# Seven weight splits moved from VectorE to accumulating DMAs, and the last heads of yB0 in another order

## The chip, the core and the metric

The kernel runs on one core of one Trainium2 chip. The core has five engines with queues of their own: TensorE (PE, matrix products; its weight loads are listed as PEld), VectorE (DVE), ScalarE (ACT), GpSimd (POOL) and SyncE (SP). Each engine works through its queue in order and waits where a semaphore tells it to. Transfers are started from a queue (here SP's, POOL's and at the very start ACT's) and then run on the core's 16 DMA engines. The metric is the time of one execution on the device in microseconds (us).

## What is computed

One layer of a block with two attention branches and a convolutional feed-forward part, on 512 tokens of width 1024, all in float32.

```python
hn = rms_norm(x, norm1_g)
proj = hn @ w_in                       # [512,1024] @ [1024,5120]
out_a = chunked_attention(qa, ka, va, q_norm_g, k_norm_g, rel_bias)   # 8 heads x 64
out_b = stick_breaking_attention(qb, kb, vb)                          # 8 heads x 64
mixed = sigmoid(gate_a) * (out_a @ w_branch_a) + sigmoid(gate_b) * (out_b @ w_branch_b)
x = x + mixed @ w_out
x = x + conv_glu(rms_norm(x, norm2_g), w_ffn_up, ffn_conv_w, ffn_conv_b, w_ffn_down)

def conv_glu(x, w_up, conv_w, conv_b, w_down):   # D_FF = 2816
    hid = causal_depthwise_conv_width_3(x @ w_up) + conv_b
    gate, up = hid[..., :D_FF], hid[..., D_FF:]
    return (silu(gate) * up) @ w_down
```

## The kernel before

**Products in three parts.** Every float32 product is built from float32r matmuls, a type with fewer bits. Each operand is split into a high half (the value cast to float32r) and a low half (the value minus its high half, cast again). `mm3` (L310) then adds three matmuls in one PSUM bank: high by high (L312), and the two mixed ones (L313, L314). So each weight has to be split on the core before TensorE can use it.

**Weights as chunks.** All weights go through one list of chunks (`CHUNKS`): the parts of `w_in`, then `yA` and `yB` (the two branch outputs, two chunks each), `wo0` to `wo3`, then `up0` to `up21` and the down projection `dn`. A chunk of up weights is a pair: 128 gate columns and the 128 up columns that belong to them, 1 MB. `load` (L124) fetches a chunk with a DMA on SP into a raw buffer [128 x 2048], of which there are two. `split_gen` (L257) splits it: ACT casts the raw weights into `whi` (L281), and DVE subtracts that from the raw weights into `wlo` (L286). In the up stage this is done in two pieces of 128 x 1024. There are two `whi` and two `wlo` buffers. When the split of chunk i is through, the load of chunk i+2 is started, into the raw buffer just read.

`run_chunk` (L301) interleaves a chunk's body with the split of the next chunk. The code order is not the order in which the engines get their instructions: a scheduler places each one by a model of how long things take, as early as its operands and buffers allow in that model, and by priority. `behind(a, b)` forbids that a is placed ahead of b on its engine; `high_priority` pulls instructions forward. So a change of engine or of modelled time for one step can reorder other engines, too.

**The second branch's last heads.** Stick-breaking attention (branch B) is done in pairs of heads. `pv` (L786) multiplies probabilities by values into a PSUM tile, then ACT copies half of it (L800), DVE adds the halves together (L801), ACT casts the result of a pair of heads into `oh_B` (L805), and DVE makes its low half `ol_B` (L806). Pairs are named by their second head: B1, B3, B5, B7. `yB_body` (L874) multiplies the four pairs by a chunk of `w_branch_b`: through `feat_groups` (L593), four groups (yB0_0 to yB0_3) of 128 features, each 4 x 3 matmuls of 512 columns in a bank of the kind MM, of which there are three. `evac` reads a finished group: DVE multiplies it by the gate `gb` (L882), adds the other branch, ACT and DVE split the sum.

**The up stage.** Three kinds of pairs. Pairs 0 and 1 run while their tokens still come in. Nine pairs (`SEVEN` = 6, 7, 9, 10, 11, 12, 13, 15, 17) run as `up_seven` (L1139): seven products of block sums in place of eight products of blocks, 84 matmuls of 256 columns (L1151), named p1 to p7. Their third to fifth weight sums were split ahead of time, parked in DRAM and are fetched by SP (`fetch_extra` L225) into `wxh` and `wxl`, or for some pairs into the buffers `w20` and `w21`. The other eleven are plain (`up_body` L1078): 48 matmuls of 512 columns through `up_mm` (L991), 24 into the bank `pg` (gate), 24 into `pu` (up); after each half ACT applies a tap of the convolution (L986) and DVE adds two more, then silu, product and, for every second pair, sums of the results for the down projection.

**POOL's queue.** In the up stage POOL does no arithmetic. It issues seven stores `ayd` of 768 KB (L1076, one after every second pair) and, from pair 18 on, the fetches `ay` of the same data (L1105).

Before the first real product, nine matmuls on a constant tile (L362, `warm`) run at the kernel's start.

Of the kernel before, what the change touches and what calls it, by code (L numbers as in the profile page):

```python
# [8 lines left out]
F32 = mybir.dt.float32  # L9
# [66 lines left out]
def block_kernel(ctx: ExitStack, tc: tile.TileContext, x, xt, params, g2, rbx, wts, wd0, wd1, out):  # L76
# [180 lines left out]
    def split_gen(i, pieces):  # L257

        if i >= len(order):
            return  # L260
        key = order[i]
        kn = CHUNKS[i][1]
        raw = raws.pop(i)
        if i - pos["up0"] in LATE and i - pos["up0"] not in LIVE:
            fetch_extra(i - pos["up0"])
        sh = 48 if key[:2] in ("qA", "kA", "vB") else 16 if key in ("up0", "up1") or is_seven(i) else 0
        n = 512 * kn if i >= FIRST_DN else 2048
        hi = wp.tile([P, 2112], F32R, tag="whi", name=f"whi_{key}")[:, sh:sh + n]
        lo = wp.tile([P, 2112], F32R, tag="wlo", name=f"wlo_{key}")[:, sh:sh + n]
        splits[key] = (hi.rearrange("p (k c) -> p k c", k=kn), lo.rearrange("p (k c) -> p k c", k=kn))  # L270
        if i >= FIRST_DN:
            yield from split_down(i - FIRST_DN, raw, hi, lo)
        elif is_seven(i):
            yield from split_seven(i, raw, hi, lo)
        n = 2048 // pieces
        cuts = CUTS[0] if i == 0 else [n * j for j in range(pieces + 1)] if i < FIRST_DN and not is_seven(i) else ()
        for j, sl in enumerate(map(slice, cuts, cuts[1:])):
            if i == 0 and j == 0:
                V.tensor_copy(hi[:, sl], raw[:, sl])
            else:  # L280
                A.copy(hi[:, sl], raw[:, sl])  # L281
                if i == 0 and j == 1:
                    yield
                    V.tensor_tensor(lo[:, 0:256], raw[:, 0:256], hi[:, 0:256].bitcast(F32), op=ALU.subtract)
            if (i, j) != (0, 0):
                V.tensor_tensor(lo[:, sl], raw[:, sl], hi[:, sl].bitcast(F32), op=ALU.subtract)  # L286
                if j < len(cuts) - 2:
                    yield


        nxt = {0: None, 1: i + 3, 2: None}.get(i - FIRST_DN, i + 2)
        if nxt is not None and nxt < len(order):
            next(load(nxt))
        j = i + 1 - pos["up0"]
        if j in SEVEN and j not in LATE:
            fetch_extra(j)
        yield
        if j in LIVE:
            yield from block_sums(i + 1)
# [9 lines left out]

    def mm3(ps, sh, sl, mh, ml, first, last):  # L310

        PE.matmul(ps, sh, mh, start=first, stop=False)  # L312
        PE.matmul(ps, sh, ml, start=False, stop=False)  # L313
        PE.matmul(ps, sl, mh, start=False, stop=last)  # L314


    hth = hp.tile([P, NK, S], F32R, tag="hth", name="hth")
# [275 lines left out]
    def feat_groups(hi, lo, name, n, kn, mh, ml, evac):  # L593
        for j in range(n):
            ps = MM(f"{name}_{j}")
            for k in range(kn):
                cs = slice(j * P, (j + 1) * P)
                mm3(ps, hi[:, k, cs], lo[:, k, cs], mh(k), ml(k), k == 0, k == kn - 1)
                if kn == 8 and k == 3:
                    yield  # L600
            evac(j, ps)
            yield
# [131 lines left out]
    def behind(ins, others):  # L734

        for o in others:
            tc.add_manual_dep(ins.ins, o.ins.name, mybir.DependencyInfo(
                mybir.DependencyClass.NoSync, mybir.DependencyReason.DATA), reason="table order")
        return ins
# [46 lines left out]
    def pv(br, h):  # L786
        ph, pl = pts.pop((br, h))
        vt = vts[f"v{br}{h // 4}"]
        ps = PV(f"pv_{br}{h}")
        for k in range(NT):  # L790
            o, n = OFF[k] + k * P, S - k * P
            for j, src in enumerate((ph, pl)):
                PE.matmul(ps[:, k * P:], vt[:, k, h % 4, :], src[:, o:o + n],
                          start=(k == 0 and j == 0), stop=(k == NT - 1 and j == 1))
        i = h % 2
        if i == 0:
            pv.o = pool_o.tile([P, S], F32, tag="of", name=f"of_{br}{h}", bufs=1)
        tmp = pool_wk.tile([P, S], F32, tag="wb", name=f"ot_{br}{h}", bufs=5)
        own, oth = ((LO, HI), (HI, LO))[i]
        A.copy(tmp[own, :], ps[oth, :])  # L800
        V.tensor_tensor(pv.o[own, :], ps[own, :], tmp[own, :], op=ALU.add)  # L801
        if i == 1:
            oh = pool_o.tile([P, S], F32R, tag="oh", name=f"oh_{br}{h}", bufs=4)
            ol = pool_o.tile([P, S], F32R, tag="ol", name=f"ol_{br}{h}", bufs=4)
            A.copy(oh, pv.o)  # L805
            V.tensor_tensor(ol, pv.o, oh.bitcast(F32), op=ALU.subtract)  # L806
            ots[br].append((oh, ol))
# [66 lines left out]
    def yB_body(i):  # L874
        def body(hi, lo):
# [3 lines left out]
            def evac(j, ps):  # L879
# [9 lines left out]
                A.copy(mh, m[:, f, :])  # L889
                V.tensor_tensor(ml, m[:, f, :], mh.bitcast(F32), op=ALU.subtract)  # L890
                mxs.append((mh, ml))
            yield from feat_groups(hi, lo, f"yB{i}", 4, 4, lambda k: o[k][0], lambda k: o[k][1], evac)
        return body

    n = 0
# [516 lines left out]
```

## Time and profile before

| what | value |
|---|---|
| median of 2 runs | 720.0 us (719.87 to 720.14) |
| the profiled execution | 719.62 us |
| its span in the profile | 717.9 us |
| PE busy | 711.6 us (99%), 3983 matmuls |
| DVE busy | 588.6 us (82%) |
| ACT busy | 410.0 us (57%) |
| POOL busy | 55.2 us (8%) |
| granted TensorE clock | 1.00 |
| data moved by DMA | 136.59 MB, 190 GB/s over the span |

How the rows are read. A page row such as "PE yB L313 <- DVE ol_B L806: 0.4, 1, 0.4" is a wait: engine, tile and line that waited, on which engine, tile and line, total us, count, longest. A timeline row is start (us from the span's start), duration, engine, line, operation, output tile <- inputs, shape, and how many alike follow; in square brackets stands what the instruction waited for. The rows of a table of windows begin with the window, its length, and then for PE, PEld, DVE, ACT and POOL the busy time with the number of instructions; behind these stand the granted clock, the busy share of the DMA engines, and GB/s. "DMA to landing" is the time from a transfer's issue to the end of its data. Matmuls overlap: a row may show 0.40 us though the next one starts 0.23 us later, so the pace is read from the starts.

In a profile, L286 is the subtraction that makes a low half of weights, L281 the cast that makes the high half, SPq L234 the second fetch for an `up_seven` pair.

### The profile page before, as it was taken

The page shows a single profiled execution, that of the slowest core. Times are in us where ns is not written, and L with a number is a line of the kernel's source. Part 1 is how long each engine was busy: PE and PEld are TensorE (multiplying, and loading weights), DVE is VectorE, ACT ScalarE, POOL GpSimd, SP SyncE. Part 2 cuts the span into 40 slices and gives each one's busy share as a digit, 9 for nine tenths or more (in the row PEclk, how much of TensorE's full clock was granted, in tenths as well). Part 3 has the DMA queues.
Part 4 walks back from the last instruction along what each step waited for, and adds up shares of the span by engine and source line. Part 5 has one row for each costly group of instructions (what it writes and reads, how often), then busy time and mean ns, then how long its engine had stood idle before and what let it go on. Part 6 is the DMA issues. An engine that isn't in the chain of part 4 may idle for free.

```text
span 717.9 us, 10814 instructions
## 1 busy us (share of the span) xinstructions
PE 711.6 (99%) x3983; PEld 619.6 (86%) x3983; DVE 588.6 (82%) x1051; ACT 410.0 (57%) x756; POOL 55.2 (8%) x91
## 2 busy tenths in 40 slices
PE   9999999999999999999999999999999999999997
PEld 7889998888988888878889988999988988888886
DVE  6678878786998998869556698999999985997687
ACT  6576657667776677544335564656655543543531
POOL 2501200000110111100003000000000100000000
PEclk9999999999999999999999999999999999999999
DMA  9722236435344444554937837667665633564563
GB/s 315 290 75 89 89 118 204 164 132 205 137 162 142 180 159 159 199 184 162 336 127 284 270 112 280 231 235 284 246 249 205 230 132 113 187 247 167 179 213 117
DMA packets 38613, 136.59 MB, mean 190 GB/s; under 512 B 4128, under 2 KB 8864, under 8 KB 31008
## 3 DMA queue, kind: packets, MB, share of 16 engines
q1 hardware_dynamic: 35616, 122.66, 47.9%
q0 software_dynamic: 2656, 13.11, 4.9%
q8 instruction: 31, 0.51, 0.3%
q14 instruction: 22, 0.18, 0.1%
q10 hardware_dynamic: 288, 0.14, 0.1%
HBM read 109.41 MB, written 26.48 MB: 189 GB/s over the span
## 4 chain that ended last, share of the span: by engine, by line
PE 97%; DVE 2%; ACT 0%; issue 0%; DVEq 0%; ACTq 0%
PE P L1245 15%; PE p L1151 12%; PE pg L313 3%; PE pg L312 3%; PE pg L314 3%; PE pu L313 3%; PE pu L314 3%; PE pu L312 3%; PE vA L443 3%; PE uA L443 3%; PE qkB L314 2%; PE gB L312 2%; PE qkB L312 2%; PE qkB L313 2%; PE gB L313 2%; PE gB L314 2%
## 5 line engine op out<-in xcount | busy, mean ns | idle before, releaser
L1245 PE MATMUL P<-whi_dn,ax 128*128 128x512 f32 x176 | 54.3, 389 | 0.0
L166 ACT CAST whi_dn<-raw_dn 128x1024 fp32r<-128x1024 f32 x33 | 34.3, 1051 | 25.8 <-PE P L1245 16.5
L162 DVE TENSOR_TENSOR wlo_dn<-raw_dn,whi_dn 128x1024 fp32r<-128x1024 f32 x33 | 40.0, 1223 | 9.5 <-ACT whi_dn L166 9.5
L314 PE MATMUL pg<-hth,wlo_up 128*128 128x512 f32 (+1 forms) x120 | 43.3, 361 | 0.0
L312 PE MATMUL pg<-hth,whi_up 128*128 128x512 f32 (+1 forms) x120 | 43.2, 361 | 0.0
L313 PE MATMUL pg<-htl,whi_up 128*128 128x512 f32 (+1 forms) x120 | 43.2, 360 | 0.0
L313 PE MATMUL pu<-htl,whi_up 128*128 128x512 f32 (+1 forms) x116 | 41.6, 359 | 0.0
L312 PE MATMUL pu<-hth,whi_up 128*128 128x512 f32 (+1 forms) x116 | 41.6, 359 | 0.0
L314 PE MATMUL pu<-hth,wlo_up 128*128 128x512 f32 (+1 forms) x116 | 41.6, 358 | 0.0
L1245 PE MATMUL P<-whi_dn,ay 128*128 128x512 f32 x132 | 40.8, 389 | 0.0
L1245 PEld LDWEIGHTS P<-whi_dn,ax 128*128 128x128 f32 x176 | 33.0, 188 | 6.8
L208 ACT CAST pkh<-pkr 128x512 fp32r<-128x512 f32 x24 | 14.9, 621 | 36.5 <-DMA parked<-pkh 15.3
L286 DVE TENSOR_TENSOR wlo_up<-raw_up,whi_up 128x1024 fp32r<-128x1024 f32 (+1 forms) x32 | 31.3, 1019 | 4.9 <-ACT whi_up L281 4.9
L1245 PE MATMUL P<-wlo_dn,ax 128*128 128x512 f32 x88 | 34.2, 389 | 0.0
L281 ACT CAST whi_up<-raw_up 128x1024 fp32r<-128x1024 f32 (+1 forms) x32 | 26.5, 886 | 10.9 <-PE pu L313 6.1
L754 POOL TENSOR_SCALAR_AFFINE_SELECT bB<-bB 128x128 f32<-128x128 f32 x32 | 18.7, 592 | 151.4 <-DVE bB L753 149.3
L1245 PEld LDWEIGHTS P<-whi_dn,ay 128*128 128x128 f32 x132 | 24.8, 188 | 5.1
L752 DVE TENSOR_TENSOR_SCAN aB<-aB,reset 128x127 f32<-128x127 f32 (+3 forms) x32 | 25.7, 813 | 4.1 <-ACT aB L747 4.1
L209 DVE TENSOR_TENSOR pkr<-pkr,pkh 128x512 fp32r<-128x512 f32 x24 | 16.4, 684 | 12.4 <-ACT pkh L208 12.4
L1245 PE MATMUL P<-wlo_dn,ay 128*128 128x512 f32 x66 | 25.8, 391 | 0.0
L312 PE MATMUL gA<-hth,whi_gA 128*128 128x512 f32 x64 | 25.5, 399 | 0.3 <-DVE mixA L632 0.3
L1151 PE MATMUL p<-ts,whi_up 128*128 128x256 f32 x144 | 25.5, 277 | 0.0
(324 smaller groups left out, 2397.6 us busy)
## 6 DMA issues: line engine op xcount, KB each, us to landing
raw_up<-in_wts SPq DMA_DIRECT2D x14, 1024.0 KB, 5.4
raw_dn<-in_wd SPq DMA_DIRECT2D x11, 1024.0 KB, 4.8
pkr<-in_wts SPq DMA_DIRECT2D x8, 1024.0 KB, 6.8
parked<-pkr SPq DMA_DIRECT2D x32, 256.0 KB, 2.5
parked<-pkh SPq DMA_DIRECT2D x24, 256.0 KB, 2.1
raw_dn<-in_wd SPq DMA_DIRECT2D x11, 512.0 KB, 3.3
ayd<-ay POOLq DMA_DIRECT2D x7, 768.0 KB, 6.3
ay<-ayd POOLq DMA_DIRECT2D x7, 768.0 KB, 6.1
```

What stands on the lines that cost most here:

```text
L162: chain("halves", V.tensor_tensor(o, x, y, op=op))
L166: chain("casts", A.copy(hi[:, sl], src))
L281: A.copy(hi[:, sl], raw[:, sl])
L286: V.tensor_tensor(lo[:, sl], raw[:, sl], hi[:, sl].bitcast(F32), op=ALU.subtract)
L312: PE.matmul(ps, sh, mh, start=first, stop=False)
L313: PE.matmul(ps, sh, ml, start=False, stop=False)
L314: PE.matmul(ps, sl, mh, start=False, stop=last)
L443: PE.matmul(pss[t], st[:, 4 * half + k, t * P:(t + 1) * P], mv[:, k, :], start=half == 0 and k == 0 and j == 0, stop=half == 1 and k == 3 ...
L752: V.tensor_tensor_scan(ar, ar, reset[:, S - n:S - 1][:, ::-1], 1.0, op0=ALU.mult, op1=ALU.max)
L754: G.affine_select(b[:, n - P:n], b[:, n - P:n], pattern=[[-1, P]], compare_op=ALU.is_gt, fill=0.0, base=0, channel_multiplier=1)
L1151: PE.matmul(ps, st, mv[:, k, :], start=first and k == 0 and n == 0, stop=last and k == 3 and n == 2, skip_group_check=True)
L1245: chain("products", PE.matmul(dst, st, mv, start=first and n == 0, stop=last and n == 2, skip_group_check=True))
```

## The change

There are two edits.

1. In `split_gen`, plain pairs from `up8` on (the test is on `up6`, and only plain pairs reach this loop: 8, 14, 16, 18, 19, 20, 21) no longer get their low halves from DVE. ACT writes the raw weights times -1 into the low buffer, whose type float32r makes that minus the high half. Then a DMA issued by POOL adds the raw weights onto it. That is two pieces for each of the seven pairs: 14 subtractions out, 14 activations and 14 accumulating DMAs of 512 KB in.

2. `yB_body` for chunk yB0 no longer uses `feat_groups`. Groups 0 to 2 get the first three pairs of heads, then these groups get the last pair (B7), and group 3 follows in a bank of another kind, SC. The first matmul of groups 1 and 2 may not be placed ahead of the last matmul of `pv`. For this, `mm3` returns its first instruction and `pv` keeps its last.

```diff
--- before.py
+++ after.py
@@ -282,7 +282,12 @@
                 if i == 0 and j == 1:
                     yield
                     V.tensor_tensor(lo[:, 0:256], raw[:, 0:256], hi[:, 0:256].bitcast(F32), op=ALU.subtract)
-            if (i, j) != (0, 0):
+            if i >= pos["up6"]:
+                A.activation(lo[:, sl], raw[:, sl], AF.Copy, scale=-1.0)
+                G.dma_start(lo[:, sl].bitcast(F32), raw[:, sl], accum_op=ALU.add)
+                if j < len(cuts) - 2:
+                    yield
+            elif (i, j) != (0, 0):
                 V.tensor_tensor(lo[:, sl], raw[:, sl], hi[:, sl].bitcast(F32), op=ALU.subtract)
                 if j < len(cuts) - 2:
                     yield
@@ -309,9 +314,10 @@
 
     def mm3(ps, sh, sl, mh, ml, first, last):
 
-        PE.matmul(ps, sh, mh, start=first, stop=False)
+        ins = PE.matmul(ps, sh, mh, start=first, stop=False)
         PE.matmul(ps, sh, ml, start=False, stop=False)
         PE.matmul(ps, sl, mh, start=False, stop=last)
+        return ins
 
 
     hth = hp.tile([P, NK, S], F32R, tag="hth", name="hth")
@@ -790,8 +796,8 @@
         for k in range(NT):
             o, n = OFF[k] + k * P, S - k * P
             for j, src in enumerate((ph, pl)):
-                PE.matmul(ps[:, k * P:], vt[:, k, h % 4, :], src[:, o:o + n],
-                          start=(k == 0 and j == 0), stop=(k == NT - 1 and j == 1))
+                pv.last = [PE.matmul(ps[:, k * P:], vt[:, k, h % 4, :], src[:, o:o + n],
+                                     start=(k == 0 and j == 0), stop=(k == NT - 1 and j == 1))]
         i = h % 2
         if i == 0:
             pv.o = pool_o.tile([P, S], F32, tag="of", name=f"of_{br}{h}", bufs=1)
@@ -889,7 +895,21 @@
                 A.copy(mh, m[:, f, :])
                 V.tensor_tensor(ml, m[:, f, :], mh.bitcast(F32), op=ALU.subtract)
                 mxs.append((mh, ml))
-            yield from feat_groups(hi, lo, f"yB{i}", 4, 4, lambda k: o[k][0], lambda k: o[k][1], evac)
+            if i == 1:
+                yield from feat_groups(hi, lo, "yB1", 4, 4, lambda k: o[k][0], lambda k: o[k][1], evac)
+                return
+            pss = [MM(f"yB0_{j}") for j in range(3)]
+            for j, ks in [(j, (0, 1, 2)) for j in range(3)] + [(j, (3,)) for j in range(3)] + [(3, range(4))]:
+                if j == 3:
+                    pss.append(SC("yB0_3"))
+                cs = slice(j * P, (j + 1) * P)
+                for k in ks:
+                    ins = mm3(pss[j], hi[:, k, cs], lo[:, k, cs], *o[k], k == 0, k == 3)
+                    if k == 0 and j in (1, 2):
+                        behind(ins, pv.last)
+                if 3 in ks:
+                    evac(j, pss[j])
+                    yield
         return body
 
     n = 0
```

The scheduler turns this into a new order on several engines. In the rows below, a row has line, operation, output tile <- inputs and shape; the number behind a tile's name is its buffer's. The lines of the new kernel are higher by 5 to 20: `mm3` is L317 to L319, `up_seven`'s products L1171, the stores L1096, the fetches L1125, the new minus halves L286 and the accumulating DMAs L287.

TensorE at the end of yB0, where the matmuls of the last pair of heads (oh_B7, ol_B7) begin, before:

```order
L313 MATMUL yB0_2_3567<-ol_B5_3223,whi_yB0_3425 128x512
L314 MATMUL yB0_2_3567<-oh_B5_3222,wlo_yB0_3426 128x512
L312 MATMUL yB0_0_3516<-oh_B7_3512,whi_yB0_3425 128x512
L312 MATMUL yB0_1_3541<-oh_B7_3512,whi_yB0_3425 128x512
L312 MATMUL yB0_2_3567<-oh_B7_3512,whi_yB0_3425 128x512
L313 MATMUL yB0_0_3516<-ol_B7_3513,whi_yB0_3425 128x512
L314 MATMUL yB0_0_3516<-oh_B7_3512,wlo_yB0_3426 128x512
L313 MATMUL yB0_1_3541<-ol_B7_3513,whi_yB0_3425 128x512
L314 MATMUL yB0_1_3541<-oh_B7_3512,wlo_yB0_3426 128x512
L313 MATMUL yB0_2_3567<-ol_B7_3513,whi_yB0_3425 128x512
L314 MATMUL yB0_2_3567<-oh_B7_3512,wlo_yB0_3426 128x512
L312 MATMUL yB0_3_3597<-oh_B1_2502,whi_yB0_3425 128x512
```

And now:

```order
L319 MATMUL yB0_2_3518<-oh_B5_3222,wlo_yB0_3426 128x512
L319 MATMUL yB0_3_3597<-oh_B5_3222,wlo_yB0_3426 128x512
L317 MATMUL yB0_0_3516<-oh_B7_3512,whi_yB0_3425 128x512
L317 MATMUL yB0_1_3517<-oh_B7_3512,whi_yB0_3425 128x512
L317 MATMUL yB0_2_3518<-oh_B7_3512,whi_yB0_3425 128x512
L317 MATMUL yB0_3_3597<-oh_B7_3512,whi_yB0_3425 128x512
L318 MATMUL yB0_0_3516<-ol_B7_3513,whi_yB0_3425 128x512
L319 MATMUL yB0_0_3516<-oh_B7_3512,wlo_yB0_3426 128x512
L318 MATMUL yB0_1_3517<-ol_B7_3513,whi_yB0_3425 128x512
L319 MATMUL yB0_1_3517<-oh_B7_3512,wlo_yB0_3426 128x512
L318 MATMUL yB0_2_3518<-ol_B7_3513,whi_yB0_3425 128x512
L319 MATMUL yB0_2_3518<-oh_B7_3512,wlo_yB0_3426 128x512
```

Before, all twelve matmuls of group yB0_3 stood behind those of the last heads. Now nine stand ahead of them (the last of these is the second row; six more are ahead of pv_B7's first matmul and two behind it), and yB0_1 and yB0_2 have moved behind pv_B7.

TensorE at the change from pair 7 (`up_seven`) to pair 8 (the first plain pair with accumulating DMAs), before:

```order
L1151 MATMUL p6_7_4858<-ts2_4528,w21_4291 128x256
L1151 MATMUL p6_7_4858<-ts2_4528,w20_4290 128x256 x2
L1151 MATMUL p6_7_4858<-ts2_4528,w21_4291 128x256
L312 MATMUL pg8_4994<-hth_102,whi_up8_4875 128x512
L313 MATMUL pg8_4994<-htl_103,whi_up8_4875 128x512
L314 MATMUL pg8_4994<-hth_102,wlo_up8_4876 128x512
L312 MATMUL pg8_4994<-hth_102,whi_up8_4875 128x512
L1151 MATMUL p1_7_4855<-hth_102,whi_up7_4756 128x256
L1151 MATMUL p1_7_4855<-htl_103,whi_up7_4756 128x256
L1151 MATMUL p1_7_4855<-hth_102,wlo_up7_4757 128x256
L1151 MATMUL p1_7_4855<-hth_102,whi_up7_4756 128x256
L1151 MATMUL p1_7_4855<-htl_103,whi_up7_4756 128x256
```

And now:

```order
L1171 MATMUL p6_7_4858<-ts2_4528,w20_4290 128x256 x2
L1171 MATMUL p6_7_4858<-ts2_4528,w21_4291 128x256
L317 MATMUL pg8_4996<-hth_102,whi_up8_4875 128x512
L318 MATMUL pg8_4996<-htl_103,whi_up8_4875 128x512
L317 MATMUL pu8_4997<-hth_102,whi_up8_4875 128x512
L318 MATMUL pu8_4997<-htl_103,whi_up8_4875 128x512
L1171 MATMUL p5_9_5062<-ts1_4453,wxh_up9_4900 128x256 x2
L1171 MATMUL p5_9_5062<-ts1_4453,wxl_up9_4901 128x256
L1171 MATMUL p5_9_5062<-ts1_4453,wxh_up9_4900 128x256 x2
L1171 MATMUL p5_9_5062<-ts1_4453,wxl_up9_4901 128x256
L1171 MATMUL p5_9_5062<-ts1_4453,wxh_up9_4900 128x256 x2
L1171 MATMUL p5_9_5062<-ts1_4453,wxl_up9_4901 128x256
```

The matmuls on pair 8's low weights (wlo_up8) have left this place. In it stand two matmuls of its other half, pu8, and then the product p5 of pair 9, which reads wxh_up9 and wxl_up9. Pair 7's p1, which began in the eighth row before, now follows behind p5_9's last two rows.

POOL's queue from the first store of the up stage on, before:

```order
L1076 DMA ayd_111<-ay0_4399 128x1536
L1076 DMA ayd_111<-ay1_4560 128x1536
L1076 DMA ayd_111<-ay2_4731 128x1536
L1076 DMA ayd_111<-ay3_4979 128x1536
L1076 DMA ayd_111<-ay4_5185 128x1536
L1076 DMA ayd_111<-ay5_5443 128x1536
L1076 DMA ayd_111<-ay6_5699 128x1536
L1105 DMA ay0_6195<-ayd_111 128x1536
L1105 DMA ay1_6197<-ayd_111 128x1536
L1105 DMA ay2_6199<-ayd_111 128x1536
L1105 DMA ay3_6201<-ayd_111 128x1536
L1105 DMA ay4_6203<-ayd_111 128x1536
```

And now:

```order
L1096 DMA ayd_111<-ay2_4731 128x1536
L287 DMA wlo_up8_4876<-raw_up8_4683 128x1024 x2
L1096 DMA ayd_111<-ay3_4981 128x1536
L1096 DMA ayd_111<-ay4_5187 128x1536
L287 DMA wlo_up14_5604<-raw_up14_5366 128x1024 x2
L1096 DMA ayd_111<-ay5_5445 128x1536
L287 DMA wlo_up16_5810<-raw_up16_5624 128x1024 x2
L1096 DMA ayd_111<-ay6_5703 128x1536
L1125 DMA ay0_6205<-ayd_111 128x1536
L287 DMA wlo_up18_6022<-raw_up18_5830 128x1024 x2
L1125 DMA ay1_6207<-ayd_111 128x1536
L287 DMA wlo_up19_6151<-raw_up19_5993 128x1024 x2
```

The pieces of pairs 8, 14, 16, 18 and 19 now stand among the stores and the first fetches; those of pairs 20 and 21 come behind ay4.

## The prediction

> **What bounds the kernel now.** I read the page's busy times first, then the waits of PE (TensorE), then a table of windows over the stage that the change edits most.
>
> ```profile
> span 717.9 us, 10814 instructions
> PE 711.6 (99%) x3983; PEld 619.6 (86%) x3983; DVE 588.6 (82%) x1051; ACT 410.0 (57%) x756; POOL 55.2 (8%) x91
> ...
> PE yB L313 <- DVE ol_B L806: 0.4, 1, 0.4
> PE gA L312 <- DVE mixA L632: 0.3, 1, 0.3
> PE yB L312 <- DVE gb L882: 0.3, 1, 0.3
> ...
> 306.00:324.00 18.00, 17.30 (x79) 13.65 (x78) 13.44 (x23) 9.74 (x17) 0.00 (x0) 1.00 0.48 173
> 576.00:594.00 18.00, 18.00 (x81) 14.92 (x80) 13.81 (x18) 8.53 (x11) 0.00 (x0) 1.00 0.37 132
> 594.00:612.00 18.00, 18.00 (x81) 14.89 (x80) 10.85 (x16) 7.78 (x11) 0.00 (x0) 1.00 0.30 107
> ```
>
> PE is busy for 711.6 of 717.9 us, and after its start it waits three times, for 1.0 us together. Of these two belong to yB, the place of the second edit. In the up stage it never waits: 81 matmuls fill 18 us, one per 0.22 us, while DVE is busy 10.85 to 13.81 us. So nothing taken off DVE there can shorten the span; the first edit can only keep the time or add waits.
>
> **The second edit (yB0).** What PE does around the last heads, and the two DVE steps it waits for:
>
> ```profile
> 316.43 0.89 PE L312 MATMUL yB<-oh_B,whi_yB 128*128 128x512 f32 x3
> 317.75 0.50 PE L313 MATMUL yB<-ol_B,whi_yB 128*128 128x512 f32 x1 [0.43 <-DVE ol_B L806]
> 318.09 0.39 PE L314 MATMUL yB<-oh_B,wlo_yB 128*128 128x512 f32 x1
> 318.32 0.39 PE L313 MATMUL yB<-ol_B,whi_yB 128*128 128x512 f32 x1
> ...
> 319.01 0.40 PE L314 MATMUL yB<-oh_B,wlo_yB 128*128 128x512 f32 x1
> 319.67 0.50 PE L312 MATMUL yB<-oh_B,whi_yB 128*128 128x512 f32 x1 [0.26 <-DVE gb L882]
> 320.01 0.40 PE L313 MATMUL yB<-ol_B,whi_yB 128*128 128x512 f32 x1
> ...
> 317.01 0.69 DVE L806 TENSOR_TENSOR ol_B<-of_B,oh_B 128x512 fp32r<-128x512 f32 x1
> ```
>
> Starts stand 0.23 apart here (318.09, 318.32). Beyond that rhythm PE loses 317.75 - 316.43 - 3 x 0.23 = 0.63, then 0.11 (317.75 to 318.09), 0.43 (319.01 to 319.67) and 0.11 (319.67 to 320.01): 1.28 us. The first pair of losses is the wait for the low half of the last heads (ol_B, done at 317.70). The second is the fourth group's wait for a bank that the first group's evacuation frees. In the new order the fourth group takes a bank of another tag, and nine of its matmuls stand ahead of the last heads. The low half is then needed at 317.1 + 10 x 0.23 = 319.4, 1.7 us after it is there, and no group waits for a bank until yB1_0, twelve matmuls after the last heads begin (318.5 + 12 x 0.23 = 321.2). The bank it needs is evacuated by about 321.0: yB0_0 ends near 320.3, plus 0.69 for an evacuation as long as L806's step. So the gain is 1.28 us. Its bounds are that, and nothing, if the evacuation comes late; I take 1.28, because both waits have a named cause that the order removes.
>
> **The first edit, per pair.** ACT, DVE and the queue that the added transfers use:
>
> ```profile
> 518.11 2.36 DVE L286 TENSOR_TENSOR wlo_up<-raw_up,whi_up 128x1024 fp32r<-128x1024 f32 x2
> ...
> 555.90 2.00 ACT L281 CAST whi_up<-raw_up 128x1024 fp32r<-128x1024 f32 x2
> 557.80 0.78 ACT L986 ACTIVATE ub<-pu,par 128x512 f32<-128x512 f32 x1
> ...
> 565.51 0.40 PE L314 MATMUL pg<-hth,wlo_up 128*128 128x512 f32 x1
> ...
> q0 software_dynamic: 2656, 13.11, 4.9%
> ...
> L1076 POOL DMA_DIRECT2D ayd<-ay x1: 539/539/539, 446.3 to 446.3; - x1
> ...
> DMA to landing us min/median/max: 3.6/3.6/3.6
> ```
>
> Removed: 14 subtractions of 2.36/2 = 1.18 us, 16.5 us of DVE, worth nothing since PE waits for none of them. Added on ACT: 14 activations of the shape of the casts, 2.00/2 = 1.0 us each, 14 us; ACT goes from 410 to 424 of 718 us. They delay the copies queued behind them by 2 us at most, and these have slack while PE works on the other pair. Added on POOL: 14 issues of 0.54 us.
>
> The unknown price is one accumulating transfer of 512 KB; no row has one. The nearest is the 768 KB store on the same queue, which landed 3.6 us after its issue. Queue 0 moved 13.11 MB in 4.9% of 16 engines' 717.9 us, so 35.2 us of all of them: 372 GB/s, or 2.1 us for 768 KB and 1.4 for 512 KB. That leaves 1.5 us fixed. Lower end: 1.5 + 1.4 = 2.9 us, as for a plain copy. Upper end: the 9.7 us of the slowest 768 KB load (row below). I take doubled data, 1.5 + 2.8 = 4.3, because an addition has to read its destination as well; it stays near the plain row of its own queue. The two pieces of a pair share the engines, so the second lands one data time later.
>
> Is it in time? Pair 18: casts 555.90 to 557.8, the tap (0.78) stands next, minus halves done at about 559.5 and 560.5. Landing 559.5 + 4.3 = 563.8 and 566.6. PE needs the first at 565.9 (565.51, and two matmuls more that were moved ahead), the second ten matmuls later, 568.2. Slack 2.1 and 1.6 us. For pair 20 the queue is the question:
>
> ```profile
> 564.72 1.61 POOL L1105 DMA_DIRECT2D ay<-ayd  x3 [16.10 <-PE p L1151]
> ...
> 575.93 2.00 ACT L281 CAST whi_up<-raw_up 128x1024 fp32r<-128x1024 f32 x2 [1.35 <-PE pu L313]
> 578.36 0.77 ACT L986 ACTIVATE ub<-pu,par 128x512 f32<-128x512 f32 x1
> ...
> 586.84 0.39 PE L312 MATMUL pg<-hth,whi_up 128*128 128x512 f32 x1
> ```
>
> Its minus halves are done at 579.7 and 580.6. Three 768 KB fetches (issued in a row with 0.54 us each) now stand behind pair 19's additions in POOL's queue, and behind their data, 3 x 2.1 = 6.3 us from about 575, follow pair 20's: done near 581.5, first addition landed near 585, second near 588. PE needs them at 586.84 + 4 x 0.23 = 587.8 and, in the new order, only after more of the pair's matmuls for the second. In time. The loads of later raw weights and of raw_dn now wait for the additions instead of the subtractions, 4 to 8 us later; each is cast a whole body (10.9 us) after, so they are hidden too. If that cover fails, ACT's casts are late next.
>
> **The wait that the change makes elsewhere.** The new order puts pair 9's second product (p5_9, from wxh_up9 and wxl_up9) ahead of pair 7's last three, four matmuls after p6_7. In the trace these weights are still on their way there:
>
> ```profile
> 459.73 1.52 PE L1151 MATMUL p<-ts,w 128*128 128x256 f32 x12
> 461.09 0.40 PE L312 MATMUL pg<-hth,whi_up 128*128 128x512 f32 x1
> ...
> 462.01 0.28 PE L1151 MATMUL p<-hth,whi_up 128*128 128x256 f32 x1
> 462.13 0.28 PE L1151 MATMUL p<-htl,whi_up 128*128 128x256 f32 x1
> ...
> 455.31 0.43 SPq L234 DMA_DIRECT2D wxl_up<-parked  x1
> ...
> DMA to landing us min/median/max: 9.7/9.7/9.7
> ...
> 458.00:461.00 3.00, 3.00 (x29) 3.00 (x28) 2.97 (x6) 3.00 (x6) 0.54 (x1) 1.00 0.96 382
> 461.00:464.00 3.00, 3.00 (x24) 2.83 (x23) 3.00 (x6) 0.59 (x3) 0.00 (x0) 1.00 1.01 409
> ```
>
> p5_9's first matmul would stand where p1_7's now stands, at 462.01, and its third, the first that reads wxl, 0.23 later at 462.24. wxl was issued at 455.31 and landed 9.7 us later, 465.0, with the DMA engines full (0.96 and 1.01). Its issue waits for nothing that the change moves. PE is in order, so it waits 2.8 us, and pair 7's products wait behind. Bounds: nothing, if the transfer is faster, to 2.8 us. I take 2.8. Pair 8's additions land behind this wait and have about 1 us more than pair 18's.
>
> **Sum.** The profiled execution took 719.6 us (span 717.9 and 1.7 around it): 719.6 - 1.3 + 2.8 = 721.1. The median of the runs is 0.4 above that execution: 721.5 us.
>
> **Rivals.** (1) The wait at p5_9 does not come, because wxl lands in time: 720.0 - 1.3 = 718.7. For it: all three of PE's waits now are under half a microsecond, so the order has so far suited the chip. Against: the landing is measured. (2) The additions are late, and the kernel is slower by over 2%. With a data time d per piece, the second piece of pair 18 lands at 559.5 + 1.5 + 2d and is needed at 568.2, so from d = 3.6 on each microsecond more costs two. Pairs 8 and 16 are built alike; the other four have longer, to about 4.3. At d = 5 that is 3 x 2 x 1.4 + 4 x 2 x 0.7 = 14 us: 735.5. It decides from d = 5, 105 GB/s, 3.5 times slower than queue 0 moves now. Between 3.6 and 5 the time is 721.5 to 735. (3) The 2.8 us wait lowers PE's clock. At the start of the trace a cold PE shows:
>
> ```profile
> 1.12 4.21 PE L362 MATMUL warm<-warm 128*128 128x512 f32 x9 [1.12 <-DVE warm L359]
> ```
>
> Nine matmuls take 4.2 us, 0.43 apart, where 0.22 apart would be 2.0: 2.2 us lost. A second cold start would give 723.7. Against it: the wait is shorter than that cold stretch, and the 0.4 us waits in yB show no slower matmuls after them. [...]
>
> **Chances.** The forecast (wait at p5_9, gain in yB, additions in time) 52%; rival 1 17%; rival 3 6%; additions late by d from 3.6 to 5, 15%; rival 2 in full 7%; the rest 3%. The range 718.5 to 727 holds the first three and nearly half of the fourth, 8 in 10; the likeliest case alone is 720.5 to 722.5. A change of 2% is about what a measurement of this kernel can tell from none: 14.4 us. Faster by that: 1%, since all of PE's waits are 1.0 us. Slower: 7%, rival 2. Within: 92%.
>
> **What would show it.** Right: PE waiting for DMA wxl_up once, near 461 to 464, for 2 to 3 us; no PE wait in yB; none for wlo_up; DVE near 572 and ACT near 424 us busy. Wrong: PE waits for the L287 transfers in several pairs (d too small), a landing of wxl before PE gets there, waits in yB1 or wo that take back the 1.28 us, or matmuls 0.43 apart after the wait.

## The result, and the profile after

| kernel | median | ratio to before, 95% interval |
|---|---|---|
| before | 720.0 us | |
| changed | 745.3 us (744.96 to 745.63, 2 runs) | 1.0349 [1.0332, 1.0366] |

The forecast was 721.5 us, within 718.5 to 727; the change costs 25.3 us. The page of the changed kernel, and under it all the waits of TensorE from 0.2 us up (engine, line and tile that waited, on what, total us, times, longest):

```profile
span 743.2 us, 10860 instructions
PE 721.2 (97%) x3983; PEld 624.0 (84%) x3983; DVE 573.6 (77%) x1037; ACT 423.1 (57%) x770; POOL 67.6 (9%) x105
q0 software_dynamic: 4672, 20.45, 10.0%
...
PE pg L319 <- DMA wlo_up<-raw_up: 11.4, 7, 3.6
PE p L1171 <- DMA wxl_up<-parked: 2.8, 1, 2.8
PE warm L368 <- DVE warm L365: 1.1, 1, 1.1
PE p L1171 <- DMA wxh_up<-parked: 1.1, 1, 1.1
PE uA L455 <- ACT whi_uA L281: 0.6, 1, 0.6
PE gA L317 <- DVE mixA L638: 0.3, 1, 0.3
PE p L1171 <- ACT pc L1179: 0.2, 1, 0.2
```

VectorE has lost 15.0 us of work and ScalarE has gained 13.1, near the 16.5 and 14 worked out. The two waits of yB are gone. But TensorE now waits 11.4 us for the additions and 3.9 for pair 9's extra weights, and its 3983 matmuls, the same number as before, are busy 9.6 us longer. A table of windows shows why, first of the kernel before, then of the changed one (window, length, then busy time and instructions of PE, PEld, DVE, ACT and POOL, then granted clock, DMA share, GB/s):

```profile
452.00:474.00 22.00, 22.00 (x157) 20.48 (x156) 21.12 (x38) 12.37 (x22) 0.54 (x1) 1.00 0.84 287
...
574.00:640.00 66.00, 66.00 (x293) 54.66 (x292) 54.04 (x73) 30.63 (x39) 1.07 (x2) 1.00 0.46 166
```

```profile
452.00:474.00 22.00, 18.11 (x127) 17.38 (x128) 12.22 (x25) 9.90 (x19) 2.33 (x3) 0.84 0.67 204
...
574.00:640.00 66.00, 54.68 (x223) 42.79 (x222) 29.45 (x44) 29.24 (x38) 7.56 (x11) 0.95 0.73 199
...
466.00:472.00 6.00, 5.61 (x26) 5.62 (x27) 0.05 (x1) 0.37 (x1) 0.88 (x1) 0.50 0.35 69
605.60:608.70 3.10, 3.10 (x7) 2.47 (x8) 0.30 (x1) 0.00 (x0) 0.88 (x1) 0.50 0.54 103
```

Most of the loss is in two places. At pair 9's p5, TensorE is idle 3.9 of 22 us, and then runs for some 6 us at a granted clock of 0.50. In the pairs 18 to 21 it is idle 11.3 of 66 us, and at a granted clock of 0.50 again behind the longest of those waits (605.60 to 608.70) and behind the last one (626.00 to 628.00). From the last `up_seven` product to the first matmul of the down projection, the stretch of these four pairs, TensorE takes 58.9 us (574.58 to 633.48); before it took 43.2 (565.39 to 608.60).

GpSimd's queue in that second place (start, duration, then what the issue waited for as far as the profile shows it):

```profile
568.42 0.90 POOL L287 DMA_DIRECT2D wlo_up<-raw_up  x1 [10.95 <-PE p L1171]
573.27 0.86 POOL L287 DMA_DIRECT2D wlo_up<-raw_up  x1 [3.95 <-ACT hg L1194]
573.86 0.85 POOL L1125 DMA_DIRECT2D ay<-ayd  x1
579.01 0.84 POOL L287 DMA_DIRECT2D wlo_up<-raw_up  x1 [4.30 <-ACT wlo_up L286]
588.07 0.86 POOL L287 DMA_DIRECT2D wlo_up<-raw_up  x1 [8.21 <-ACT whi_up L281]
588.60 0.89 POOL L1125 DMA_DIRECT2D ay<-ayd  x1
593.82 1.09 POOL L1125 DMA_DIRECT2D ay<-ayd  x2 [4.33 <-issue]
600.97 0.90 POOL L287 DMA_DIRECT2D wlo_up<-raw_up  x1 [6.06 <-issue]
```

ScalarE, which wrote the minus halves, and the load of pair 20's raw weights:

```profile
566.97 2.00 ACT L286 ACTIVATE wlo_up<-raw_up 128x1024 fp32r<-128x1024 f32 x2
576.68 2.00 ACT L286 ACTIVATE wlo_up<-raw_up 128x1024 fp32r<-128x1024 f32 x2
588.72 1.99 ACT L286 ACTIVATE wlo_up<-raw_up 128x1024 fp32r<-128x1024 f32 x2
...
578.84 0.33 SPq L149 DMA_DIRECT2D raw_up<-in_wts  x1
```

Both minus halves of pair 18 are written by 569.0. The first addition is issued at 568.42 and lands after 4.5 us, at 572.9. The second is issued only then, at 573.27, though its data had been ready for 4.3 us, and lands 5.4 us later, at 578.7. That frees the raw buffer, so at 578.84 SP starts the next 1 MB load. At 579.01, 0.3 us after the same landing, GpSimd issues pair 19's first addition. It is in flight together with that load, which lands at 585.3, and takes 8.7 us instead of 4.5. The releasers in brackets (such as "ACT hg") had long been done. What stands 0.3 us ahead of every start here but 568.42 and the fetches at 573.86 and 588.60 is the landing of an earlier transfer of this queue. The 600.97 follows the first fetch of 593.82, which took 6.8 us.

### The profile page after: what moved, and what is told of

Same layout as the page of the kernel before. It is cut to its first block, busy times and chain, and to the rows that moved or that the text cites. A ratio compares the mean times of both kernels' runs of the same rounds, so it can differ in the third digit from the quotient of the medians.

```text
span 743.2 us, 10860 instructions
## 1 busy us (share of the span) xinstructions
PE 721.2 (97%) x3983; PEld 624.0 (84%) x3983; DVE 573.6 (77%) x1037; ACT 423.1 (57%) x770; POOL 67.6 (9%) x105
## 4 chain that ended last, share of the span: by engine, by line
PE 85%; DMA 7%; DVE 3%; ACT 2%; issue 2%; SPq 0%; POOL 0%; DVEq 0%; ACTq 0%; POOLq 0%
PE P L1265 13%; PE p L1171 8%; DMA wlo_up<-raw_up 3%; PE vA L449 3%; PE pg L319 3%; DMA wxl_up<-parked 3%; PE uA L449 3%; PE pg L317 2%; PE pg L318 2%; PE pu L319 2%; PE pu L318 2%; PE pu L317 2%; PE qkB L319 2%; PE gB L317 2%; PE qkB L317 2%; PE qkB L318 2%
## 5 line engine op out<-in xcount | busy, mean ns | idle before, releaser
L319 PE MATMUL pg<-hth,wlo_up 128*128 128x512 f32 (+1 forms) x120 | 45.5, 379 | 11.5 <-DMA wlo_up<-raw_up 11.4
L317 PE MATMUL pg<-hth,whi_up 128*128 128x512 f32 (+1 forms) x120 | 44.1, 368 | 0.0
L319 PE MATMUL pu<-hth,wlo_up 128*128 128x512 f32 (+1 forms) x116 | 42.0, 362 | 0.0
L317 PE MATMUL pu<-hth,whi_up 128*128 128x512 f32 (+1 forms) x116 | 41.9, 361 | 0.0
L319 PEld LDWEIGHTS pg<-hth,wlo_up 128*128 128x128 f32 x120 | 23.1, 192 | 18.2 <-DMA wlo_up<-raw_up 14.9
L208 ACT CAST pkh<-pkr 128x512 fp32r<-128x512 f32 x24 | 14.9, 621 | 31.8 <-DMA parked<-pkh 14.2
L1006 ACT ACTIVATE cg<-pg,par 128x512 f32<-128x512 f32 x13 | 10.1, 777 | 36.7 <-DVE ub L1091 19.2
L162 DVE TENSOR_TENSOR raw_dn<-raw_dn 128x512 f32<-128x512 f32 x22 | 15.2, 689 | 18.8 <-DMA raw_dn<-in_wd 18.4
L318 PEld LDWEIGHTS pg<-htl,whi_up 128*128 128x128 f32 x120 | 23.1, 192 | 3.6
```

What stands on the lines that cost most here:

```text
L162: chain("halves", V.tensor_tensor(o, x, y, op=op))
L208: A.copy(hi, b[o])
L317: ins = PE.matmul(ps, sh, mh, start=first, stop=False)
```

## The experiments

A time below without a number of runs is that of one execution. Beside each of them the kernel before took 720.3 to 720.4 us.

**The two edits apart.** One kernel keeps only yB0's new order:

```diff
-            if i >= pos["up6"]:
...
-            elif (i, j) != (0, 0):
+            if (i, j) != (0, 0):
                 V.tensor_tensor(lo[:, sl], raw[:, sl], hi[:, sl].bitcast(F32), op=ALU.subtract)
```

> Only the second edit (yB0's order); the low halves of all pairs stay with VectorE. The profile of the changed kernel has no TensorE wait in yB any more, and its matmuls there lose 1.25 us less than before. Theory A (the second edit gains what it takes out of yB): 718.7 us, 0.998 of before. Theory B (the gain is given back later, in yB1 or wo): 720.0.

Measured: 718.87 us (11 runs), ratio 0.9982 [0.9973, 0.9991]. No wait of TensorE in yB. The other kernel keeps only the first edit, with `feat_groups` back in `yB_body`:

> Only the first edit (minus halves by ScalarE, additions by DMA), yB0 in the old order. If the two edits don't act on each other, the 745.3 us of the changed kernel plus 1.3: 746.6 us. If the second edit has a part in the loss (by another order in the up stage), under 743.

Measured: 743.96 us, beside 720.3 for the kernel before. That is between the two forecasts: its waits for wlo_up are 12.3 us, but it waits only 1.5 for wxl_up and not for wxh_up, and it has 1.6 us of waits for VectorE at the start of the down projection that the changed kernel doesn't have. So the second edit is a gain of its own and the loss is there without it. How much of it falls at pair 9 differs from run to run (below).

**Plain copies in place of additions.**

```diff
-                G.dma_start(lo[:, sl].bitcast(F32), raw[:, sl], accum_op=ALU.add)
+                G.dma_start(lo[:, sl].bitcast(F32), raw[:, sl])
```

> The changed kernel with plain copies in place of the accumulating transfers: the same bytes written, the same order on TensorE and GpSimd. The addition is left out, so the low halves of seven pairs are the raw weights. Theory A (room: GpSimd's queue holds three plain 128-row transfers, as the four fetches of before show, and an accumulating one takes the room of two, so the second piece of a pair can't be issued before the first has landed): the second piece is issued 0.6 us after the first, both land within 5 us, and nearly all TensorE waits for wlo_up (11.4 us and the slow matmuls behind them, 17 us in all) are gone; the wait for wxl_up9 stays: 728 us, 726 to 731. Theory B (any two transfers into one pair's low halves are issued one after the other): the second piece is still issued only after the first has landed, 2.9 us instead of 4.2; over 735 us.

Measured: 725.06 us. TensorE waits no more for wlo_up, and still 3.9 us at pair 9. GpSimd's queue at pair 14, in this kernel and then in the changed one:

```profile
523.83 0.53 POOL L287 DMA_DIRECT2D wlo_up<-raw_up  x1 [16.07 <-ACT wlo_up L286]
524.78 0.53 POOL L287 DMA_DIRECT2D wlo_up<-raw_up  x1 [0.42 <-ACT wlo_up L286]
```

```profile
525.85 0.89 POOL L287 DMA_DIRECT2D wlo_up<-raw_up  x1 [16.05 <-ACT wlo_up L286]
530.74 0.87 POOL L287 DMA_DIRECT2D wlo_up<-raw_up  x1 [4.00 <-ACT hg L1194]
```

The second copy is issued 0.95 us after the first, as soon as ScalarE is through; the second addition 4.89 us after the first. The wait is a matter of the addition, not of two writes into one tile. Theory A holds; the time is 0.9 us under its range.

**Additions of 64 rows.**

```diff
-                G.dma_start(lo[:, sl].bitcast(F32), raw[:, sl], accum_op=ALU.add)
+                for r in (slice(0, 64), slice(64, P)):
+                    G.dma_start(lo[r, sl].bitcast(F32), raw[r, sl], accum_op=ALU.add)
```

> Each accumulating transfer of 128 rows cut into two of 64 rows (28 of 256 KB in place of 14 of 512 KB), nothing else. Theory A (room by rows: 64 accumulated rows take half the room): two of them are in flight together, the second issued under 1 us after the first, before it has landed; the third waits for a landing. Time near that of the changed kernel, 740 to 750 us. Theory B (accumulating transfers run strictly one at a time, whatever their size): each is issued 0.6 us after the one before has landed, four times 3.5 us per pair: over 755 us.

Measured: 755.72 us. The queue at pair 14:

```profile
523.63 2.58 POOL L288 DMA_DIRECT2D wlo_up<-raw_up  x3 [16.03 <-ACT wlo_up L286]
528.54 0.81 POOL L288 DMA_DIRECT2D wlo_up<-raw_up  x1 [2.33 <-issue]
```

Three are issued in a row, so these additions didn't run one at a time. The fourth comes 0.3 us after the landing of the first, 4.6 us after its issue, at 528.2. Theory A holds but for its count, which was off by one: three of 64 rows were in flight together. The time is theory B's for another reason: the data are slower. Queue 0 is at 12.2% of 754.0 us here, 10.0% of 743.2 in the changed kernel, for the same bytes. At this pair the last quarter lands 10.2 us after its issue, so the pair takes 15.1 us (523.63 to 538.7) where two additions of 128 rows took 9.5 (525.85 to 535.3). But SP issued a load of 768 KB at 528.66, right behind the last quarter, which the changed kernel issues only behind the pair (535.82); so a part of this may be that load.

**One addition of 1 MB for each pair.**

```diff
-                G.dma_start(lo[:, sl].bitcast(F32), raw[:, sl], accum_op=ALU.add)
+                if j == len(cuts) - 2:
+                    G.dma_start(lo.bitcast(F32), raw, accum_op=ALU.add)
```

> The changed kernel with one accumulating transfer of 1 MB (rows of 8 KB) for each pair in place of two of 512 KB, issued once both minus halves are written. Theory A (room counts rows, not bytes): it takes the room of two, one fetch or store may be in flight with it, and it lands 1.5 + 2 x 2.8 = 7.1 us after its issue where no load is in the way; both pieces come then, against 4.2 and 9.1 us now. Pairs 18 to 21 gain little: 738 to 748 us. Theory B (room counts bytes): it isn't issued while any other transfer of GpSimd is in flight; over 750.

Measured: 745.96 us. Its shortest landing is 7.0 us, and at pairs 18 and 19 the queue shows:

```profile
572.75 0.88 POOL L288 DMA_DIRECT2D wlo_up<-raw_up  x1 [0.19 <-DVE ub L1092]
582.96 0.88 POOL L288 DMA_DIRECT2D wlo_up<-raw_up  x1 [9.34 <-issue]
583.52 0.90 POOL L1126 DMA_DIRECT2D ay<-ayd  x1
594.25 1.08 POOL L1126 DMA_DIRECT2D ay<-ayd  x2 [9.83 <-issue]
```

One fetch goes beside an addition of 1 MB (583.52), as one went beside an addition of 512 KB in the changed kernel (573.86 behind 573.27). The second one comes only at 594.25, 0.3 us after the landing of the addition (11.0 us after 582.96). That is theory A's outcome. And without the wait between the two pieces the time is the same. So that wait alone isn't the loss. (The first half of the weights now comes as late as the second, so this run doesn't price the wait by itself.)

**Half of the additions.** The second piece of each pair goes back to VectorE:

```diff
-            if i >= pos["up6"]:
+            if i >= pos["up6"] and j == 0:
```

> The changed kernel, but only the first piece of each of the seven pairs by an addition; the second by VectorE's subtraction as before. No piece then waits for room behind the other one of its pair. Theory A (the second piece's wait for the first is the root of the late low halves): the TensorE waits for wlo_up (11.4 us) fall under 2, the wait for wxl_up9 stays; 745.3 - 15 = 730 us, 726 to 733. Theory B (an addition alone is too late, since it lands 8.5 us after its issue where a raw load stands ahead of it): over 737.

Measured: 720.68 us. The waits for wlo_up are 1.1 us in all, and the stretch of pairs 18 to 21 takes 44.3 us instead of 58.9. Theory A's mechanism holds. The time is better than it gave because there is no wait for wxl_up9: it landed after 7.7 us, and the order at p5 isn't that of the changed kernel. Twelve products of pair 7 now stand between p5's first products with wxh_up9 (461.38) and the one with wxl_up9 (463.02). So this run is a test of the low halves, not of p5.

**Groups of pairs.** The condition is replaced by a list: pair 8 alone, pairs 14 and 16, pairs 18 to 21.

```diff
-            if i >= pos["up6"]:
+            if i - pos["up0"] in (18, 19, 20, 21):
```

> The second edit, and the additions in pairs 18 to 21 alone. In the changed kernel TensorE loses 15.6 us more than before between 574 and 640 us. Theory A (these pairs make a chain of their own: second piece after the first has landed, next raw load after the second, next first piece behind that load): 718.9 + 15.6 = 734.5 us. Theory B (they are late because pairs 8 to 16 were): under 728.

Measured: 736.22 us, with 11.6 us of waits for wlo_up. The stretch of these four pairs takes 59.4 us, as long as in the changed kernel (58.9). Theory A holds: these four pairs are late by themselves.

> The second edit, and the additions in pairs 14 and 16 alone. In the changed kernel TensorE loses 1.75 us more than before between 522 and 574 us. Theory A (each such pair pays for its own second piece, and these two have an up_seven pair ahead of them, which gives them time): 718.9 + 1.7 = 720.6 us, waits for wlo_up under 1.5 us. Theory B (all plain pairs pay alike, as four of them pay 17 us): 718.9 + 2 x 4.3 = 727.5.

Measured: 725.17 us, nearer to theory B. Pair 14's second addition landed 7.8 us after its issue, and TensorE waited 4.5 us in two times. In the changed kernel, where these pairs lost little, the wait at pair 9 had held TensorE up ahead of them; that this gave the additions time was not tried.

> The second edit, and the additions in pair 8 alone; the six other plain pairs keep VectorE's subtractions. In the changed kernel TensorE loses 7.1 us between 450 and 474 us: 4.2 in the waits for wxh_up9 and wxl_up9, the rest in matmuls that start 0.21 us apart instead of 0.11 behind them. Theory A (all of that comes from where pair 9's p5 stands): 718.9 + 7.1 = 726.0 us, with the same two waits. Theory B (it is the load that the additions put on the DMA engines): the waits shrink under 1 us; 720.

Measured: 722.31 us in one run; no wait for wxl_up9. The same kernel again:

> The kernel with additions in pair 8 alone once more, now timed several times. Its profile had no wait for wxl_up9, which landed 6.9 us after its issue there, and 10.8 in the changed kernel. Theory A (this landing differs from run to run, and the wait with it): times spread over 721 to 727 us. Theory B (it is the same in every run of one kernel): all within 1 us of 722.3.

Measured: 724.02 us, 720.44 to 726.88 in 10 runs; the kernel before beside it, 719.89 to 720.82 in 13. Theory A holds. In this profile, of 726.88 us, wxl_up9 landed 11.5 us after its issue and p5 waited 2.8; in the first one it landed after 7.2 (the expectation says 6.9). A late landing doesn't need the additions: with the second edit alone, which has none, it took 10.8 us. Against the 718.9 us of the second edit alone, the three groups cost 5.1, 6.3 and 17.4 us, 28.8 together; all seven pairs cost 26.4.

**Pair 9's p5 kept back.**

```diff
+                        if j == 9 and ps is b5 and first and k == 0 and n == 0:
+                            behind(ins, late["seven_end"])
+                        if j == 7:
+                            late["seven_end"] = [ins]
```

> The changed kernel with pair 9's p5 kept behind pair 7's last matmul. Theory A (its wait for wxl_up9 was a loss of its own): that wait and the slow matmuls behind it are gone, 745.3 - 7.1 = 738 us. Theory B (it covered pair 8's late additions, of which the first landed at 468.9 and the second at 473.8 us; TensorE would now want them from 467 on): waits for wlo_up8 of 4 us take its place; 742 us.

Measured: 755.55 us, worse than both. Pair 8's second addition landed 9.0 us after its issue, and TensorE waited 6.1 us for it in the place of p5's wait, as theory B has it. But the waits for wlo_up grew to 19.9 us over the whole up stage, and one addition of pair 16 moved behind a store. Of the 10 us above the changed kernel, 7.2 lie ahead of pair 18, and 4.1 between the first matmul of the down projection and the end (113.8 us against 109.7). Why the down projection got longer was not tried.

**The fetches behind the additions.** ay2 to ay4 are issued after pair 21's last addition:

```diff
-        G.dma_start(ay, ayd[i])
+        ins = G.dma_start(ay, ayd[i])
+        if 2 <= i < 5:
+            behind(ins, [late["acc"]])
```

> The changed kernel with the fetches ay2 to ay4 kept behind the last addition in GpSimd's queue; before they stood ahead of pair 20's additions. Theory A (the fetches' places in the queue delay pair 20: in the changed kernel its minus halves were written by 590.7 and its first addition was issued at 600.97, after ay3 had landed): that addition is issued near 594, right after pair 19's second has landed, and the waits of pairs 20 and 21 (3.7, 1.5 and 2.0 us, and the slow matmuls behind them) shrink: 737 to 741 us. Theory B (the raw loads and the serial additions alone set the pace of these pairs): 744 to 746.

Measured: 736.67 us. The queue from pair 19's first addition to pair 21's first:

```profile
573.20 0.84 POOL L287 DMA_DIRECT2D wlo_up<-raw_up  x1 [4.29 <-ACT wlo_up L286]
582.31 0.87 POOL L287 DMA_DIRECT2D wlo_up<-raw_up  x1 [8.28 <-ACT whi_up L281]
587.75 0.85 POOL L287 DMA_DIRECT2D wlo_up<-raw_up  x1 [4.57 <-issue]
596.83 0.86 POOL L287 DMA_DIRECT2D wlo_up<-raw_up  x1 [8.23 <-issue]
601.64 0.85 POOL L287 DMA_DIRECT2D wlo_up<-raw_up  x1 [3.95 <-ACT wlo_up L286]
```

The stretch of pairs 18 to 21 takes 56.9 us here (568.78 to 625.63) instead of 58.9, so the fetches cost some 2 us (theory A, in part). Most of the rest of the gain lies ahead of these pairs, at p5: the waits for wxl_up were 1.2 us in this run, and there was none for wxh_up. What stays is the pace of the additions: from 573.20 over 587.75 to 601.64, 14.2 us per pair.

## Why the prediction was wrong

**The step that failed** is in the price of an addition: "The two pieces of a pair share the engines, so the second lands one data time later." The size of one addition was right. Alone it lands after 4.5 to 4.6 us (4.3 taken). Queue 0's share gives 0.100 x 743.2 - 35.2 = 39.1 us for 14 additions, 2.8 each, as taken. (The copies of the same bytes: 0.075 x 723.4 - 35.2 = 19.1 us, 1.4 each, and the shortest of them landed after 2.9 us, the prediction's lower end.) What the second half of an addition's time goes to, for which the prediction named a read of the destination, no run shows. But no two of them were in flight together in the changed kernel. The fence of before that the prediction quoted for its pair 20 held the hint: three fetches issued in a row at 564.72, of which the first landed 4.6 us later, and the fourth not before this:

```profile
569.59 0.54 POOL L1105 DMA_DIRECT2D ay<-ayd  x1 [3.26 <-issue]
```

In the traces of before and of the changed kernel GpSimd never had more in flight than three plain transfers, or one addition and one plain transfer. A pair's second addition was issued 0.3 us after the first had landed, in all seven pairs, where at pair 14 the second copy went out 0.95 us behind the first (copy). At that pair the second addition lands 9.5 us after the first's issue instead of 7.1. (The issues were mis-sized, too: 0.87 us each and not 0.54, which nothing waited for.)

**The second failed step** follows from it: the later raw loads come "4 to 8 us later", "so they are hidden too". Pair 20's load started at 578.84 instead of 560.57. Of these 18.3 us, 8.5 are the time by which pair 18's casts began later (564.39 instead of 555.90); the other 9.8 are the additions'. The load itself was in time: it landed after 6.5 us, at 585.3, and the cast at 586.15 waited for TensorE. What the prediction had left out is what the load does to the next addition. It starts at 578.84, behind the same landing (578.7) that this addition follows at 579.01, so the two are in flight together, and the addition takes 8.7 us. So a pair's additions occupy the queue for 4.6 + 8.7 us and two issues 0.3 us behind a landing, 13.9 us (14.2 measured with the fetches away; in the changed kernel the three steps from 568.42 to 610.71, between the first additions of pairs 18, 19, 20 and 21, are 14.1 each on average). A plain pair has 48 matmuls at 0.228 us, 10.9 us. Where plain pairs follow each other, at 18 to 21, the additions set the pace. Pair 20, for which the prediction had the additions landed "near 585" and "588", got its first one issued at 600.97. How long TensorE takes for these four pairs, from the last `up_seven` product to the first matmul of the down projection, says the same:

| kernel | pairs 18 to 21 |
|---|---|
| before | 43.2 us |
| copies in place of additions (copy) | 42.8 us |
| half of the additions (half) | 44.3 us |
| fetches behind the additions (fetch_behind) | 56.9 us |
| changed | 58.9 us |
| additions in these pairs alone (p18_21) | 59.4 us |
| one addition of 1 MB per pair (one1m) | 59.5 us |

Taking away half of the additions ends the loss. Taking away only the wait between them doesn't: an addition of 1 MB carries as much data per pair and meets the load as well (7.0 us at its shortest, 11.0 for the one issued at 582.96, behind a load at 582.70). Which share of the loss is the missing overlap and which the meeting with the load was not separated.

**Rival 2** named this outcome, slower by late additions, but put its threshold at the data time ("from d = 3.6 on"). It came at d = 2.8, because neither the missing overlap nor the knock-on from pair to pair was in its formula.

**The wait at p5** was right in place and size, 2.8 us for wxl_up9, with 1.1 for wxh_up9 that was left out. But it comes in one execution and not in the next, with the same kernel (p8). The single landing of 9.7 us in the trace of before was one draw: of the fourteen traces of this case, six have 7.2 to 8.1 us and eight 9.7 to 11.5. So rival 1, that the wait doesn't come, was too low at 17%, and that it came in the profiled execution was in part luck.

**Rival 3** came too, at 6% and 2.2 us. After the two waits at p5 the granted clock was 0.50 from 466 to 472, and so it was behind the wait of 3.6 us at 605.59, but not behind the one of 2.7 us at 593.55, where the starts are 0.23 us apart and not 0.43:

```profile
593.55 0.50 PE L319 MATMUL pg<-hth,wlo_up 128*128 128x512 f32 x1 [2.74 <-DMA wlo_up<-raw_up]
593.89 0.40 PE L317 MATMUL pg<-hth,whi_up 128*128 128x512 f32 x1
594.12 0.40 PE L318 MATMUL pg<-htl,whi_up 128*128 128x512 f32 x1
...
605.59 0.80 PE L319 MATMUL pg<-hth,wlo_up 128*128 128x512 f32 x1 [3.56 <-DMA wlo_up<-raw_up]
606.18 0.63 PE L317 MATMUL pg<-hth,whi_up 128*128 128x512 f32 x1
606.61 0.63 PE L318 MATMUL pg<-htl,whi_up 128*128 128x512 f32 x1
```

The length of one wait alone doesn't sort these cases. In the changed kernel the granted clock was also 0.50 from 626.00 to 628.00, 1.5 us after a wait of only 1.87 us, and 1.00 from 593.50 to 596.50, behind the 2.74 us. With the fetches behind the additions (fetch_behind) the matmuls start 0.43 us apart at once behind 2.77 us, almost the length that left them alone at 593.55:

```profile
624.49 0.50 PE L319 MATMUL pg<-hth,wlo_up 128*128 128x512 f32 x1 [1.87 <-DMA wlo_up<-raw_up]
...
626.01 0.63 PE L319 MATMUL pg<-hth,wlo_up 128*128 128x512 f32 x1
626.43 0.63 PE L317 MATMUL pg<-hth,whi_up 128*128 128x512 f32 x1
```

```profile
616.37 0.80 PE L319 MATMUL pg<-hth,wlo_up 128*128 128x512 f32 x1 [2.77 <-DMA wlo_up<-raw_up]
616.96 0.63 PE L317 MATMUL pg<-hth,whi_up 128*128 128x512 f32 x1
617.39 0.63 PE L318 MATMUL pg<-htl,whi_up 128*128 128x512 f32 x1
```

So the prediction's argument against rival 3, that the wait is shorter than the 4.2 us of slow matmuls at the start, failed not only because a wait of 1.1 us stood just ahead of the 2.8: slow matmuls followed waits of 1.87, 2.77 and 3.56 us as well. What else decides, such as where the wait falls in time, these runs don't settle.

**What was right:** the second edit (1.28 us forecast; 718.87 against 720.3 measured), DVE and ACT busy times, and that VectorE's relief is worth nothing here: half, with 7 of the 14 subtractions gone, takes 720.68 us and isn't faster than the second edit alone (718.87).

## What to carry to other kernels

A transfer's price is not only its data time: count what it occupies in its issuer's queue, and what its landing releases. Here two additions of 2.8 us of data each took 14.2 us per pair in GpSimd's queue (fetch_behind), where TensorE has work for 10.9. Before work is moved from a compute engine to DMAs, lay out one period of the stage (issue, landing, next issue, next load) and compare it with the bound engine's time for the same period. Taking work off an engine that nobody waited for paid nothing here (half: 720.68 us, against 718.87 without the additions). And a wait read from one landing time in a busy stretch is a chance, not a fact: the landing of wxl_up9 took 7.2 us in one execution of a kernel and 11.5 in another (p8, p8_again).

## What the runs showed of the hardware that was not expected

- GpSimd's next issue came 0.3 us after a landing, without a semaphore wait that would explain the stall, when three 128-row transfers were in flight (before: the third issued at 565.78, a landing at 569.27, the next issue at 569.59), or one addition and one transfer (changed kernel: the second issued at 588.60, a landing at 593.51, the next issue at 593.82). Of additions of 64 rows, three were in flight together (rows64, from 523.63). Beside one addition of 1 MB, in rows of 8 KB, there was one fetch (one1m, 583.52), as beside one of 512 KB, in rows of 4 KB (changed kernel, 573.86).
- A 512 KB addition issued just behind a 1 MB load of SP's queue landed after 8.7 us instead of 4.5 (8.7 in the changed kernel, 8.8 twice in fetch_behind).
- Additions of 64 rows are slower for the same bytes: by queue 0's share (0.122 x 754.0 - 35.2 = 56.8 us) they took 4.1 us per 512 KB, an estimate, where those of 128 rows took 2.8.
- The landing of wxl_up9 differs between executions of one kernel: 7.2 us in the one of 722.31 us, 11.5 in the one of 726.88. That kernel's times go from 720.4 to 726.9 us.
- TensorE's granted clock was 0.50 from 1.5 us after a wait of 1.87 us (changed kernel, 626.00 to 628.00), and matmuls started 0.43 us apart right behind one of 2.77 us (fetch_behind, 616.96); behind one of 2.74 us it was 1.00 (changed kernel, 593.50 to 596.50).
